# Down projection of a streaming encoder: later bias preparation, another order of the three form slots, and the last part of x added in DRAM

## The chip, the cores and the metric

The kernel runs on one core of a Trainium2 chip. A core has a matrix engine (PE, with its weight loads shown as PEld), a vector engine (DVE), a scalar engine (ACT), a general engine (POOL, which also issues DMAs) and SP, which only issues DMAs. Each engine works through its own list of instructions in order; so does each DMA queue's issuer. The metric is the device time of one launch in microseconds (us), lower is better.

## The reference, cut to what matters

One step of a hybrid encoder, here with one layer of each of its two kinds; all in float32, for 1024 prompt frames and 8 x 16 sample frames (nine tiles of 128 rows, D = 1024).

```python
def rmsnorm(x, g):
    return x * rsqrt(mean(x * x, -1) + 1e-6) * g

def mlp(x, g_norm, w_up, w_down):            # w_up 1024x4096, w_down 4096x1024
    return square(relu(rmsnorm(x, g_norm) @ w_up)) @ w_down

# layer 0: sliding-window attention with distance penalty and sinks
hp = hp + band_attention(...) @ w_o_a
hp = hp + mlp(hp, g_mlp[0], w_up[0], w_down[0])
# layer 1: shared K/V, own queries, learned bias on the clipped distance
k_b, v_b = shared_kv(hp, g_kv, w_kv, g_k_b)
s = q @ k_b.T / 8 + table[clip(q_pos - k_pos, -128, 128) + 128]
hp = hp + softmax(s) @ v_b @ w_o_b
hp = hp + mlp(hp, g_mlp[1], w_up[1], w_down[1])   # hp, hs are outputs
```

## The kernel before

Each of the two layers runs `attention`, `wo_phase`, `mlp_up` and `mlp_down`. A float32 product is done as three products of rounded parts (high x high, high x low, low x high: `mm3`), so every operand is first split: ACT writes the high part, DVE the rest (`split`, L128 and L134).

`mlp_down` multiplies the 4096-wide activations by `w_down` with a scheme that needs 20 block products where plain blocking needs 24, run twice over (two halves `s` of the inner dimension): 40 **products**, numbered n = 0 to 39, in an order that `CHAINS` fixes. A product reads a **form** (a combination of activation blocks that `mlp_up` left in DRAM as `hd`) and a combination of weight blocks. It has three PSUM banks of 12 matmuls each, 36 matmuls in all.

- Forms come by SP (`load_h`, L1023) into three slots a0, a1, a2, 768 KB each. `slot(n)` is n % 3, but slot 1 for n = 39. A slot can be loaded again when the product that reads it has ended; at the end of iteration n the loop issues the next form whose slot is not claimed by a nearer one. Then ACT casts the form (L128) and DVE makes its low part (L134).
- Weight blocks come by SP into r slots (1 MB each, `load_w`). `add_w` sums two of them on DVE (L1059) two products ahead; `split_w` splits the sum (ACT L128, DVE L134) one product ahead. All loads of this function are held in one order by `self.sp`; most of its DVE work is held in one order by `self.dve` (`chain`). Everything else is ordered by a scheduler that takes ready instructions by program order, with a lead of 1000 for the start of the next layer's attention.
- The result has three **parts** of three token tiles each (part 0 is tiles 5, 6, 7; part 1 is 2, 3, 4; part 2 is the sample tile, 0, 1), each in two column halves. Where a part's x tiles aren't open yet, a bank is copied by ACT into an o slot (L1151) and added to DRAM (`xp`) by one accumulating DMA of POOL (L1165, 768 KB). Part 2 is opened after product 1 and part 1 after product 12 (`X_AT`): their first write is an ACT copy (L1157), later ones DVE adds (L1159); when the last has come, POOL adds each tile (512 KB) to DRAM (L1092), after product 30 for part 2, 35 for part 1. Part 0 (`HELD`) is opened after product 34 by three SP loads of x from DRAM; products 37 (left half) and 39 (right half) are added by DVE, and SP stores the tiles (L1090). In the second layer POOL also copies parts 1 and 2 from DRAM to the output (L1170) three products after their end.

The nine x tiles, the slots and the next layer's attention share SBUF; a tile of the next stage can be written once every old tile under it is given back. Counted from the pools of the program, in bytes per partition: x5, x6, x7 lie at 52800 to 65088, x8 and x0 (part 2) at 91200 to 99392, x1 at 118336 to 122432; a0 at 106048, a1 at 138816, a2 at 151104, each 12288 long. In the second layer's attention, the normed and transposed first tile `hh` lies at 92224 to 96320 and `hl` at 96320 to 100416 (written at L128 and L134 from `ps_n`), a bias tile `biasB` at 116800, `gk`, `gq` at 120896, the first piece of the second tile at 121920; the weights `wq` over x6 and x7. In `mlp_up`, the first sum of x (`sx0`) lies under a0 and is last read by the first product of the last block; under a2 lie `sx4` and the sample's x8, last read when the sample products of that block have ended.

`prep_bias` (L1185) prepares the second layer's distance bias while the first layer's `mlp_down` runs: it loads a table (`tb`), clears `fr` and `big` and makes differences on DVE, stores `fr` to `fd`, writes it 128 times over to `rd` in DRAM (3072 KB, L1196), then gathers 16 pieces of `rd` into `big` (L1210, L1212) and stores that (`biasSd`). In the program it stands ahead of product 20 (`RANK`), but nothing orders it.

At the seam of the layers the second layer's first loads and splits (`w_kv` by L146, POOL L185, DVE L190) stand between the last products; after product 39 PE transposes x (L210), `hh` and `hl` are split, and the K/V products begin (L217 to L219).

Of the kernel before, what the change touches and what calls it, by code (L numbers as in the profile page):

```python
# [16 lines left out]
P = 128  # L17
# [6 lines left out]
KV = 4  # L24
# [70 lines left out]
class Build:  # L95
# [869 lines left out]
    def mlp_down(self, layer, out):  # L965
# [3 lines left out]
        with ExitStack() as st:  # L969
# [46 lines left out]
            last = {i // 2: max(left[i], left[i ^ 1]) for i in left}  # L1016
            aa, ws = {}, {}

            def slot(n):
                return 1 if n == total - 1 else n % 3  # L1020
# [57 lines left out]
            fresh_x = set()  # L1078

            def start_x(i):  # L1080
                for t in PARTS[i]:
                    xs[t] = take(f"x{t}")
                    if i == HELD:
                        load(xs[t], self.xd[t])
                    else:
                        fresh_x.update((t, h) for h in range(2))

            def store_x(i, t):
                if i == HELD:
                    nc.sync.dma_start(out(t), xs[t])  # L1090
                    return
                nc.gpsimd.dma_start(self.xd[t], xs[t], accum_op=ALU.add)  # L1092
                if out(t) is not self.xd[t]:
                    copies.append((n + 3, t))

            copies = []
# [22 lines left out]
            for n, (s, p, g, first, final, reads, _) in enumerate(seq):  # L1119
                if layer == 0 and n == RANK:  # L1120
                    self.prep_bias(self.dp)
                if n + AHEAD < total:
                    load_w(n + AHEAD)
# [8 lines left out]
                adds = {}  # L1132
                for o, v in reads:
                    if PARTS[o // 2][0] not in xs:
                        adds[o] = take(f"o{no % 2}")
                        no += 1
                for i in range(3):
# [11 lines left out]
                    for o, v in reads:  # L1149
                        if o in adds:  # L1150
                            nc.scalar.activation(adds[o][:, i], banks[i], AF.Copy, scale=float(v))  # L1151
# [3 lines left out]
                        if (t, o % 2) in fresh_x:  # L1155
                            fresh_x.remove((t, o % 2))
                            nc.scalar.activation(x, banks[i], AF.Copy, scale=float(v))  # L1157
                            continue
                        chain(tt(x, x, banks[i], ALU.add if v > 0 else ALU.subtract))  # L1159
                    for part in {o // 2 for o, _ in reads}:  # L1160
                        if last[part] == n:
                            store_x(part, PARTS[part][i])
                for o, z in adds.items():
                    dst = self.xp[o // 2][:, :, N[o % 2]].rearrange("t p n -> p t n")
                    nc.gpsimd.dma_start(dst, z, accum_op=ALU.add)  # L1165
                if n in X_AT:
                    start_x(X_AT[n])
                for m, t in copies:
# [719 lines left out]
```

## Time and profile before

| | us |
|---|---|
| median of 3 runs | 2364.53 (2361.72 to 2369.41) |
| the profiled execution, whole | 2373.72 |
| its span, first to last instruction | 2371.9 |
| PE busy in the span | 2284.4 |
| first layer's `mlp_down`, products 0 to 39 | 804.5 to 1150.4 |
| its products 20 and 37 begin at | 976.9 and 1117.5 |
| second layer's, products 0 to 39 | 2032.4 to 2367.5 |

The page gives busy times, the chain of work that ended last, and the costliest groups. "[2.69 <-DVE w L134]" behind a row of the timeline is idle time of the engine ahead of that instruction and what ended it. In the rows of the chain the columns are start, length, what. A row of the table by stretches gives for each engine the busy time and, in brackets, the number of instructions that began there, then PEclk (the granted clock of PE, 1.00 is full), the DMA engines' busy share and GB/s.

### The profile page before, as it was taken

The numbers are of one execution on the slowest core, as the hardware profiler recorded it, in microseconds if no ns is written. First come the engines' busy times: TensorE is split into PE (matmuls) and PEld (weight loads), VectorE is DVE, ScalarE is ACT, GpSimd is POOL, SyncE is SP. The second block draws the span as 40 slices with busy tenths as digits, with TensorE's granted clock in tenths as the row PEclk, the third lists the DMA queues.
The fourth block names the chain that finished last, engine by engine and source line by source line (L and its number), as shares of the span: only waits on it lengthen the run. The fifth ranks groups of instructions, "written<-read, shape, count | busy, mean of one in ns | idle before, by whom it ended". The sixth has DMA issues, their size and how long they took to land.

```text
span 2371.9 us, 33381 instructions
## 1 busy us (share of the span) xinstructions
PE 2284.4 (96%) x11429; PEld 1903.3 (80%) x11429; DVE 1723.7 (73%) x3084; ACT 1326.7 (56%) x2675; POOL 626.0 (26%) x938
## 2 busy tenths in 40 slices
PE   7998999899999999999999999998899999999998
PEld 6787877788888877887777788877788888888887
DVE  6788786666656578898577876777665565678886
ACT  3777675555555555444377666665555555554442
POOL 4334332313213111002233434344132132210010
PEclk9999999999999999999999999999999999999999
DMA  7335546234434798649553655555244343977465
GB/s 253 116 118 161 177 141 208 83 121 161 136 113 153 219 270 191 212 129 240 184 157 109 198 151 175 171 165 182 65 158 137 116 156 111 286 202 210 168 176 170
DMA packets 226042, 394.27 MB, mean 166 GB/s; under 512 B 51496, under 2 KB 126192, under 8 KB 225776
## 3 DMA queue, kind: packets, MB, share of 16 engines
q1 hardware_dynamic: 189680, 288.30, 38.1%
q0 software_dynamic: 34896, 99.11, 15.1%
q10 hardware_dynamic: 1296, 4.72, 0.5%
q8 instruction: 90, 1.47, 0.3%
q14 instruction: 80, 0.66, 0.1%
HBM read 238.08 MB, written 156.07 MB: 166 GB/s over the span
## 4 chain that ended last, share of the span: by engine, by line
PE 72%; DVE 9%; DMA 8%; ACT 4%; issue 4%; POOL 2%; SPq 0%; ACTq 0%; POOLq 0%; DVEq 0%
PE ps_c L743 6%; PE ps_c L744 6%; PE ps_c L745 6%; PE ps_x L743 5%; PE ps_x L745 5%; PE ps_x L744 5%; PE ps_mm L217 3%; PE ps_mm L219 3%; PE ps_mm L218 3%; DMA a<-hd 3%; PE ps_y L745 2%; PE ps_y L743 2%; PE ps_y L744 2%; PE ps_tr L324 2%; DVE w L134 2%
## 5 line engine op out<-in xcount | busy, mean ns | idle before, releaser
L743 PE MATMUL ps_c<-w,a 128*128 128x512 f32 x960 | 377.1, 393 | 8.8 <-DVE x L1159 5.7
L744 PE MATMUL ps_c<-w,a 128*128 128x512 f32 x960 | 376.6, 392 | 8.6 <-DVE w L134 8.6
L745 PE MATMUL ps_c<-w,a 128*128 128x512 f32 x960 | 375.9, 392 | 0.0
L908 POOL DMA_DIRECT2D hd<-h x272 | 148.8, 550 | 595.7 <-ACT h L817 373.5
L743 PEld LDWEIGHTS ps_c<-w,a 128*128 128x128 f32 x960 | 181.7, 189 | 51.2 <-DVE x L1159 5.7
L744 PEld LDWEIGHTS ps_c<-w,a 128*128 128x128 f32 x960 | 181.7, 189 | 48.2 <-DVE w L134 10.7
L128 ACT CAST a<-a 128x1536 fp32r<-128x1536 f32 x80 | 118.6, 1483 | 167.3 <-DMA a<-hd 167.3
L745 PEld LDWEIGHTS ps_c<-w,a 128*128 128x128 f32 x960 | 181.7, 189 | 37.9
L134 DVE TENSOR_TENSOR a<-a 128x1536 fp32r<-128x1536 f32 x80 | 140.2, 1753 | 63.9 <-ACT a L128 63.6
L217 PE MATMUL ps_mm<-w,hh 128*128 128x512 f32 x432 | 173.9, 404 | 6.4 <-POOL w L185 2.5
L219 PE MATMUL ps_mm<-w,hl 128*128 128x512 f32 x432 | 173.2, 402 | 2.1 <-DMA hl<-hTd 1.9
L218 PE MATMUL ps_mm<-w,hh 128*128 128x512 f32 x432 | 172.4, 400 | 1.7 <-DVE w L190 1.6
L743 PE MATMUL ps_x<-sx,w 128*128 128x512 f32 (+1 forms) x408 | 159.4, 391 | 3.5 <-ACT h L864 2.5
L128 ACT CAST w<-ru 128x512 fp32r<-128x512 f32 (+1 forms) x160 | 110.0, 708 | 83.7 <-PE ps_y L744 32.0
L745 PE MATMUL ps_x<-sx,w 128*128 128x512 f32 (+1 forms) x408 | 155.7, 382 | 0.0
L744 PE MATMUL ps_x<-sx,w 128*128 128x512 f32 (+1 forms) x408 | 155.6, 381 | 0.0
L128 ACT CAST w<-s 128x2048 fp32r<-128x2048 f32 x56 | 107.1, 1913 | 86.6 <-DVE s L1059 75.8
L134 DVE TENSOR_TENSOR w<-s,w 128x2048 fp32r<-128x2048 f32 x56 | 128.1, 2288 | 31.8 <-ACT w L128 30.8
L1165 POOL DMA_DIRECT2D xp<-o x28 | 36.1, 1289 | 419.0 <-ACT o L1151 407.9
L134 DVE TENSOR_TENSOR ptl<-ps_tr,pth 128x512 fp32r<-128x512 f32 x180 | 122.3, 685 | 26.4 <-ACT pth L128 20.7
L134 DVE TENSOR_TENSOR w<-ru,w 128x512 fp32r<-128x512 f32 (+1 forms) x160 | 126.6, 793 | 14.7 <-ACT w L128 14.6
L816 ACT ACTIVATE h<-h 128x512 f32<-128x512 f32 (+1 forms) x102 | 61.9, 607 | 123.3 <-DVE h L866 93.3
(271 smaller groups left out, 6135.5 us busy)
## 6 DMA issues: line engine op xcount, KB each, us to landing
a<-hd SPq DMA_DIRECT2D x80, 768.0 KB, 5.3
hd<-h POOLq DMA_DIRECT2D x272, 192.0 KB, 2.5
ru<-in_w_up SPq DMA_DIRECT2D x64, 512.0 KB, 4.0
r<-in_w_down SPq DMA_DIRECT2D x32, 1024.0 KB, 11.0
xp<-o POOLq DMA_DIRECT2D x28, 768.0 KB, 9.5
x<-xp SPq DMA_DIRECT2D x29, 512.0 KB, 4.6
o<-oTd SPq DMA_DIRECT2D x50, 256.0 KB, 5.3
xp<-xo SPq DMA_DIRECT2D x18, 512.0 KB, 2.9
```

The costliest lines, as they stand in the source:

```text
L128: a = nc.scalar.copy(hi, src)
L134: return a, e.tensor_tensor(lo, src, hi.bitcast(F32), ALU.subtract)
L217: nc.tensor.matmul(ps, a, w[:, 0, k, :], start=(k == 0), stop=False)
L218: nc.tensor.matmul(ps, a, w[:, 1, k, :], start=False, stop=False)
L219: self.lp = nc.tensor.matmul(ps, b, w[:, 0, k, :], start=False, stop=(k == KC - 1))
L324: self.lp = nc.tensor.transpose(pt[:, i, :], get(i), self.ident)
L743: a = mm(ps, ah, bh, start=first, stop=False, skip_group_check=True)
L744: mm(ps, ah, bl, start=False, stop=False, skip_group_check=True)
L745: return a, mm(ps, al, bh, start=False, stop=last, skip_group_check=True)
L816: a = nc.scalar.activation(t, src, AF.Relu)
L908: return lambda p, z: self.nc.gpsimd.dma_start(self.hd[c // 4][:, p, c % 4], z)
L1165: nc.gpsimd.dma_start(dst, z, accum_op=ALU.add)
```

## The change

Bias preparation: the table's load follows the last load of forms or weights that was issued, the two clears follow the DVE chain (so none can run ahead of product 20), `big` is cleared with them, and the 16 gathers and the store of `biasSd` become `spread_bias`, called ahead of product 24, each gather after the last load issued by then.

Form slots: n % 3 throughout; in the first layer turned by one, so that products 0, 1, 2 use a2, a0, a1 and 37, 38, 39 use a0, a1, a2. In the second layer 37, 38, 39 use a1, a2, a0.

Part 0: in the first layer it is never opened. ACT copies each bank of products 37 and 39 into the matching half of x8, x0, x1 (part 2's tiles, stored after product 30), and POOL adds that half (256 KB) to DRAM: six accumulating DMAs in the place of three loads, six DVE adds and three SP stores. In the second layer only the left half (product 37) goes that way, and POOL copies it to the output at iteration 38; the right half is loaded after product 33, added by DVE at product 39 and stored by SP, 256 KB a tile.

```diff
@@ -1013,11 +1013,12 @@
             for n, (s, *_, reads, _) in enumerate(seq):
                 for i, _ in reads:
                     left[i] = n
-            last = {i // 2: max(left[i], left[i ^ 1]) for i in left}
+            last = [max(left[2 * i], left[2 * i + 1]) for i in range(3)]
+            opened = {}
             aa, ws = {}, {}
 
             def slot(n):
-                return 1 if n == total - 1 else n % 3
+                return n % 3 if layer else (n + 2) % 3
 
             def load(dst, src):
                 a = nc.sync.dma_start(dst, src)
@@ -1075,25 +1076,28 @@
             def early(n):
                 return self.tc.high_priority(EARLY[n]) if n < len(EARLY) else nullcontext()
 
-            fresh_x = set()
-
-            def start_x(i):
-                for t in PARTS[i]:
-                    xs[t] = take(f"x{t}")
-                    if i == HELD:
-                        load(xs[t], self.xd[t])
-                    else:
-                        fresh_x.update((t, h) for h in range(2))
-
-            def store_x(i, t):
-                if i == HELD:
-                    nc.sync.dma_start(out(t), xs[t])
-                    return
-                nc.gpsimd.dma_start(self.xd[t], xs[t], accum_op=ALU.add)
-                if out(t) is not self.xd[t]:
-                    copies.append((n + 3, t))
-
-            copies = []
+            def start_x(n):
+                for o in X_AT[layer].get(n, ()):
+                    opened[o] = n
+                    for t in PARTS[o // 2]:
+                        if t not in xs:
+                            xs[t] = take(f"x{t}")
+                        if o == HELD:
+                            load(xs[t][:, N[o % 2]], self.xd[t][:, N[o % 2]])
+
+            def store_x(o, t):
+                if o == HELD and o in opened:
+                    nc.sync.dma_start(out(t)[:, N[1]], xs[t][:, N[1]])
+                elif o // 2 and last[o // 2] == n:
+                    nc.gpsimd.dma_start(self.xd[t], xs[t], accum_op=ALU.add)
+
+            def copy_x(n):
+                for part in range(3):
+                    for t in PARTS[part] if layer else ():
+                        if part and last[part] + 3 == n:
+                            nc.gpsimd.dma_start(out(t), self.xd[t])
+                        elif not part and left[0] + 1 == n:
+                            nc.gpsimd.dma_start(out(t)[:, N[0]], self.xd[t][:, N[0]])
 
             for n in range(AHEAD):
                 with early(n):
@@ -1119,6 +1123,8 @@
             for n, (s, p, g, first, final, reads, _) in enumerate(seq):
                 if layer == 0 and n == RANK:
                     self.prep_bias(self.dp)
+                if layer == 0 and n == RANK + 4:
+                    self.spread_bias(self.dp)
                 if n + AHEAD < total:
                     load_w(n + AHEAD)
                 split_h(n + 1)
@@ -1129,10 +1135,15 @@
                 if first:
                     banks = [self.psum("c", [P, 512], "ps_c") for _ in range(3)]
                 a, w = aa.pop(n), ws.pop(n)
-                adds = {}
+                adds, whole = {}, {}
                 for o, v in reads:
-                    if PARTS[o // 2][0] not in xs:
-                        adds[o] = take(f"o{no % 2}")
+                    if o not in opened:
+                        if n > max(last[1:]) + 1:
+                            adds[o] = [xs[t][:, N[o % 2]] for t in PARTS[2]]
+                            continue
+                        z = take(f"o{no % 2}")
+                        adds[o] = [z[:, i] for i in range(3)]
+                        whole[o] = z
                         no += 1
                 for i in range(3):
                     if i == 2 and n + 2 in total_of:
@@ -1148,26 +1159,26 @@
                     self.follow(z[0][0], z[-1][1])
                     for o, v in reads:
                         if o in adds:
-                            nc.scalar.activation(adds[o][:, i], banks[i], AF.Copy, scale=float(v))
+                            nc.scalar.activation(adds[o][i], banks[i], AF.Copy, scale=float(v))
+                            if o not in whole:
+                                dst = self.xd[PARTS[o // 2][i]][:, N[o % 2]]
+                                nc.gpsimd.dma_start(dst, adds[o][i], accum_op=ALU.add)
                             continue
                         t = PARTS[o // 2][i]
                         x = xs[t][:, N[o % 2]]
-                        if (t, o % 2) in fresh_x:
-                            fresh_x.remove((t, o % 2))
+                        if opened[o] is not None and o != HELD:
                             nc.scalar.activation(x, banks[i], AF.Copy, scale=float(v))
+                            if i == 2:
+                                opened[o] = None
                             continue
                         chain(tt(x, x, banks[i], ALU.add if v > 0 else ALU.subtract))
-                    for part in {o // 2 for o, _ in reads}:
-                        if last[part] == n:
-                            store_x(part, PARTS[part][i])
-                for o, z in adds.items():
+                    for o in {o // 2: o for o, _ in reads if left[o] == n}.values():
+                        store_x(o, PARTS[o // 2][i])
+                for o, z in whole.items():
                     dst = self.xp[o // 2][:, :, N[o % 2]].rearrange("t p n -> p t n")
                     nc.gpsimd.dma_start(dst, z, accum_op=ALU.add)
-                if n in X_AT:
-                    start_x(X_AT[n])
-                for m, t in copies:
-                    if m == n:
-                        nc.gpsimd.dma_start(out(t), self.xd[t])
+                start_x(n)
+                copy_x(n)
                 for _, z in zip(range(LATER), late):
                     chain(z)
                 for m in range(n + 1, total):
@@ -1185,8 +1196,10 @@
         nc = self.nc
         with ExitStack() as st:
             tb, fr, big = self.tb, self.fr, self.big
-            nc.sync.dma_start(tb, self.ins["rel_bias_b"][0])
-            nc.vector.memset(fr, 0.0)
+            a = nc.sync.dma_start(tb, self.ins["rel_bias_b"][0])
+            self.behind(self.sp, a)
+            self.behind(self.dve, nc.vector.memset(fr, 0.0))
+            self.behind(self.dve, nc.vector.memset(big, BIG))
             nc.vector.tensor_scalar(
                 fr[:, 127:383], tb[:, 256:0:-1], -1.0, tb[:, 256:257], ALU.mult, ALU.add
             )
@@ -1203,15 +1216,20 @@
                 )
 
             self.fsrc = fsrc
-            nc.vector.memset(big, BIG)
-            for h4 in range(G):
-                for b in range(2):
-                    r = slice(h4 * 32 + b * 16, h4 * 32 + b * 16 + 16)
-                    nc.sync.dma_start(big[r, :, b * P : b * P + P], fsrc(h4, 0, 16, KV, G, P))
-                    c = 256 + b * 16
-                    nc.sync.dma_start(big[r, :, c : c + 16], fsrc(h4, P, 16, KV, G, 16))
-            self.biasSd = dp.tile([KV, P, 288], F32, tag="biasSd", name="biasSd")
-            nc.sync.dma_start(self.biasSd[0:KV].rearrange("j p c -> p j c"), big)
+
+    def spread_bias(self, dp):
+        nc, big, fsrc = self.nc, self.big, self.fsrc
+        for h4 in range(G):
+            for b in range(2):
+                r = slice(h4 * 32 + b * 16, h4 * 32 + b * 16 + 16)
+                c = 256 + b * 16
+                for z in (
+                    nc.sync.dma_start(big[r, :, b * P : b * P + P], fsrc(h4, 0, 16, KV, G, P)),
+                    nc.sync.dma_start(big[r, :, c : c + 16], fsrc(h4, P, 16, KV, G, 16)),
+                ):
+                    self.behind(self.sp, z)
+        self.biasSd = dp.tile([KV, P, 288], F32, tag="biasSd", name="biasSd")
+        nc.sync.dma_start(self.biasSd[0:KV].rearrange("j p c -> p j c"), big)
 
     def prep_gains(self):
         nc, I = self.nc, self.ins
@@ -1831,8 +1849,8 @@
 TAIL = 6
 LATER = 3
 AHEAD = 3
-X_AT = {1: 2, 12: 1, 34: 0}
-HELD = 0
+X_AT = ({1: (4, 5), 12: (2, 3)}, {1: (4, 5), 12: (2, 3), 33: (1,)})
+HELD = 1
 WO_ORDER = [[0, 4, 1, 5, 2, 6, 7, 3, ST], [0, 4, 1, 5, 6, 2, 7, 3, ST]]
 
 CFG = [
```

## Prediction

> **What bounds the kernel now.** I read the page first, then the chain of waits, then tables by stretches around every product of the two down projections.
>
> ```profile
> span 2371.9 us, 33381 instructions
> PE 2284.4 (96%) x11429; PEld 1903.3 (80%) x11429; DVE 1723.7 (73%) x3084; ACT 1326.7 (56%) x2675; POOL 626.0 (26%) x938
> PE 72%; DVE 9%; DMA 8%; ACT 4%; issue 4%; POOL 2%; SPq 0%; ACTq 0%; POOLq 0%; DVEq 0%
> ```
>
> PE is the bound, and the chain of waits leaves it for 28% of the span: there another engine or a transfer sets the pace. The change touches only the down projections and the seam behind the first one, so I looked for products that are longer than the rest.
>
> ```profile
> core 0: us, PE busy (x) PEld busy (x) DVE busy (x) ACT busy (x) POOL busy (x), PEclk, DMA share, GB/s
> 870.46:878.62 8.16, 8.16 (x38) 6.76 (x37) 4.61 (x3) 3.11 (x3) 0.00 (x0) 1.00 1.01 297
> 878.62:911.58 32.96, 26.55 (x109) 21.24 (x108) 19.18 (x12) 15.84 (x16) 3.86 (x3) 0.95 0.87 217
> 1108.89:1131.85 22.96, 19.83 (x73) 15.41 (x73) 20.16 (x18) 6.82 (x6) 8.31 (x10) 0.85 0.88 244
> 1140.02:1150.41 10.39, 8.57 (x37) 6.81 (x37) 3.85 (x4) 0.00 (x0) 0.00 (x0) 1.00 0.31 112
> 2354.57:2367.50 12.93, 10.24 (x37) 7.67 (x35) 4.40 (x4) 0.00 (x0) 0.00 (x0) 0.87 0.19 77
> ```
>
> The first row is an undisturbed product (8 of the first layer): 8.16 us. The others: products 9 to 11, 8.48 above three such; 36 and 37, 6.64 above two; 39 of the first layer, 2.23 above one; 39 of the second, 4.77 above one, with PE idle for only 2.69 of it: the rest is clock (PEclk 0.87).
>
> **The change part by part.** The sum is made against the profiled execution (span 2371.9, whole 2373.72, 9.2 above the median 2364.53); I carry the difference over to the median.
>
> *The last product of the second layer.*
>
> ```profile
> 2346.61 5.49 DMA a<-hd
> 2352.12 1.49 ACT a L128
> 2353.63 1.76 DVE a L134
> 2355.39 2.21 DVE w L134
> ...
> 2367.54 0.69 DVE x L1159
> ```
> ```profile
> 2344.56 2.28 DVE L1059 TENSOR_TENSOR r<-r,r 128x2048 f32<-128x2048 f32 x1
> ```
> ```profile
> 2357.65 0.50 PE L744 MATMUL ps_c<-w,a 128*128 128x512 f32 x1 [2.69 <-DVE w L134]
> ```
>
> Form 39 shares slot 1 with product 37 and is loaded when that has ended; load, cast and two low parts make 10.95 us, more than product 38's 8.16. With three slots it follows product 36, one product earlier (at the end of 36, 2346.41 - 8.16 = 2338.3), lands by 2343.8 and is cast by 2345.3. The weights' sum ends at 2346.84; ACT's cast of it (near 2 us) and the two low parts, 1.76 and 2.21, are done by some 2352.8, ahead of 2354.57, where the product begins. What is late next is nothing until PE itself. Of 4.77 some 0.2 is the end of the last matmul: **-4.5**, and nothing in the queue can undo it (ends -4.6 and -3.5).
>
> A sentence of the Trainium skill speaks against the clock's share: TensorE: Matmul & The Clock Gate, section Why this matters for your kernels, names idle gaps over some 3 us as what drops the clock. Here 2.69 us idle already comes with a granted clock of 0.87, so the trace disagrees; by the rule this term would be an estimated -2.9.
>
> *The last store* moves 256 KB a tile, not 512. The last add ends at 2368.23, the span 3.67 later; the smallest near row is 2.5 (hd<-h, below). **-0.5** (ends -1.2 and 0). The left half's accumulation (512 KB take 8.9, below) and its copy fall under products 38 and 39, 16 us of cover; without it they would stand behind the end, at 8.9 and more.
>
> *Product 39 of the first layer* waits for the same load: **-2.2** (ends -2.2 and 0, if DVE is held by the seam's work instead).
>
> *Product 37 of the first layer.*
>
> ```profile
> 1104.76 1.18 DVE L190 SCALAR_TENSOR_TENSOR w<-raw,gcol,w 128x512 fp32r<-128x512 f32 x1 [1.50 <-POOL w L185]
> ...
> 1116.90 1.84 DVE L190 SCALAR_TENSOR_TENSOR w<-raw,gcol,w 128x512 fp32r<-128x512 f32 x2 [0.68 <-POOL w L185]
> 1118.67 2.28 DVE L134 TENSOR_TENSOR w<-r,w 128x2048 fp32r<-128x2048 f32 x1
> ```
>
> The next layer's weight splits (L190) stand on DVE ahead of w(36) and w(37), and DVE stood 1.50 us for POOL, which waited for the w_kv load; that load stood behind the three x loads (1.5 MB), which go. So w(37) comes up to 1.50 earlier, and product 37's wait, of at least 1.5, roughly halves; clock losses shrink faster than waits (2.23 above for the first layer's 39, 4.77 for the second's). A full working gives -4.2; the order on DVE may differ, so I take **-3.0** (ends -6.6, all of it, and +3, as much again as the wait).
>
> *The bias preparation.*
>
> ```profile
> 870.69 14.81 DMA a<-hd
> 885.52 1.49 ACT a L128
> 887.03 1.76 DVE a L134
> 888.79 2.20 DVE w L134
> ```
> ```profile
> 865.88 0.32 SPq L1194 DMA_DIRECT2D fd<-fr  x1
> 867.38 0.60 SPq L1196 DMA_DIRECT2D rd<-fd  x1
> ...
> 882.63 0.33 SPq L1210 DMA_DIRECT2D big<-rd  x1
> ...
> 896.09 0.44 SPq L1212 DMA_DIRECT2D big<-rd  x1
> ...
> 901.85 0.38 SPq L1214 DMA_DIRECT2D biasSd<-big  x1
> ```
> ```profile
> L1189 DVE MEMSET fr<- x1: 378/378/378, 862.1 to 862.1; 16x384 f32 x1
> ...
> L1206 DVE MEMSET big<- x1: 1018/1018/1018, 862.7 to 862.7; 128x1152 f32 x1
> ...
> L1190 DVE TENSOR_SCALAR fr<-tb x1: 336/336/336, 865.5 to 865.5; 16x256 f32<-16x256 f32 x1
> ```
> ```profile
> 978.31 0.69 DVE L1159 TENSOR_TENSOR x<-x,ps_c 128x512 f32<-128x512 f32 x1 [4.53 <-ACT x L1157]
> ...
> 981.12 0.68 DVE L1159 TENSOR_TENSOR x<-x,ps_c 128x512 f32<-128x512 f32 x1
> ...
> 1007.46 0.68 DVE L1159 TENSOR_TENSOR x<-x,ps_c 128x512 f32<-128x512 f32 x1
> ```
>
> Although it stands at product 20, it ran at product 7: rd is written in 15 us (867.38 to the first gather at 882.63), form 10 lands only 2.9 us behind it, and products 9 to 11 lose 8.48. Tied down, it runs from product 20 on (976.9 here). There DVE works almost without a gap from 978.31 to 1007.46, so the two clears and the difference, 0.38 + 1.02 + 0.34 = 1.74 us, come straight on the path of w(21) to w(23); ahead of them stands the add at 981.12, so fr is ready near T20 + 6.7 (T20: begin of product 20) and rd goes out near T20 + 8.4. SP's next form, 23, becomes free for issue at the same time. If it goes behind rd it lands near T20 + 25 (form 10 landed 18.1 after rd went out, with the DMA engines full; a little less here). Product 23 could begin at T20 + 3 x 8.16 + 1.74 = T20 + 26.2, and cast and low parts (1.49 + 1.76 + 2.2) want the form 5.5 ahead of that, at T20 + 20.8: 4.2 us of wait and, as in the second layer's last product, some 1.6 of clock. The 16 gathers take SP 13.5 us (882.63 to 896.09) from product 24 on and push form 27, due at 8.16, by 5.3 us. Its slack is two products less load and parts, 16.3 - 5.5 - 5.5 = 5.3: 0.2. biasSd waits until 901.85, another 5.3 on SP; behind it stands form 28, whose place comes up by then. Sum after: 1.74 + 4.2 + 1.6 + 0.2 = 7.7, against 8.48: **-0.8**. Bounds: 2.0 if form 23 goes first (-6.5); form 27 behind biasSd as well (+6: 5.3 of wait and some clock). The nearest row is this same transfer, so I stay by it.
>
> *The seam.*
>
> ```profile
> 1151.05 2.08 ACT L128 CAST hh<-ps_n 128x512 fp32r<-128x512 f32 x4 [11.08 <-PE ps_n L210]
> ```
> ```profile
> 1152.20 0.48 PE L217 MATMUL ps_mm<-w,hh 128*128 128x512 f32 x1
> ```
> ```profile
> hd<-h POOLq DMA_DIRECT2D x272, 192.0 KB, 2.5
> ...
> xp<-x POOLq DMA_DIRECT2D x12, 512.0 KB, 8.9
> ```
>
> Here the change adds a wait. hh and hl lie on x8 and x0. Before, these tiles were given back after product 30, and the cast ran 0.64 us behind product 39 (end E = 1150.41). Now x0 carries bank 1 of product 39: its matmuls end at E - 2.7 (a third of a product), a copy like DVE's 0.69 ends near E - 1.8, and POOL's accumulation must land first. No 256 KB accumulation is in the trace; it lies between 2.5 (192 KB, plain) and 8.9 (512 KB, added): I take 5, between the two. So hh is free near E + 3.2, the K/V products begin near E + 4.6 instead of E + 1.8: 2.8, and 1.2 of clock for a PE pause of that length (1.9 stood behind 2.69): **+4.0** (ends +1 and +9). Behind the cast ACT holds only later tiles; behind gk and gq on SP (x1, free near E + 6) stand the w_q loads, which are needed after the K/V products of three tiles only.
>
> *The first products of the first layer.*
>
> ```profile
> 788.14 8.64 DMA a<-hd
> ```
> ```profile
> 793.31 0.40 PE L743 MATMUL ps_x<-sx,w 128*128 128x512 f32 x1
> ```
>
> Form 0 goes to a2 and must wait for the end of the sample products (793.31), 5.2 us later than 788.14. But the 1 MB ahead of it has then landed: 5.5 as in the calm load above, so 798.8 against 796.8. Cast and low parts, 5.5, end at 804.3; product 0 began at 804.5. It just fits: **+0.3** (ends 0 and +2).
>
> The first layer's six ACT copies and POOL issues in the place of DVE adds lie beside PE's products 37 to 39, where ACT is idle for most of the time (0.00 busy in the last product's row).
>
> Sum: -4.5 - 0.5 - 2.2 - 3.0 - 0.8 + 4.0 + 0.3 = **-6.7**, so 2364.5 - 6.7 = 2357.8.
>
> **The rivals.** *The bias finds a gap* (form 23 ahead of rd): -6.5 for -0.8, sum -12.4, 2352.1. For: the two are ready within 1 us of each other. Against: rd stands first in the program.
>
> *The wait only changes its place:* product 37 stays as it is and the seam costs 9 (an accumulation like the 8.9 row): -4.5 - 0.5 - 2.2 - 0.8 + 9 + 0.3 = +1.3, 2365.8. Then the change doesn't do what it says for the first layer. For: most accumulations of the page take that long. Against: DMA share 0.31 in the last product.
>
> *Slower, by POOL's queue.* The accumulations of product 37 wait on POOL for ACT; if the scheduler puts w_kv's splits (L185) behind them, DVE's L190 wait for POOL, and w(38) and w(39) stand behind those: two stalls like that of 37 (about 6.2 each, 6.64 with product 36's share), 37 itself as before. That is two times 6.2 for 38 and 39, of which 2.2 was there before at 39: -4.5 - 0.5 - 0.8 + 4 + 0.3 + 12.4 - 2.2 = +8.7, 2373.2. It decides from the point where a split block is queued behind bank 2 of product 37. For: the 1.50 and 0.68 waits above are of this kind. Against: the splits have a lead of 1000 in the order.
>
> **How the numbers follow.** Forecast 0.44, with its own range 2352 to 2363; bias in a gap 0.24; changed place 0.16; slower 0.16. A measurement of this kernel can tell about 0.3% (7.1 us) from no change, so the forecast itself lies on that edge: 0.23 of it faster, 0.21 within. Faster 0.23 + 0.24 = 0.47; within 0.21 + 0.16 = 0.37; slower 0.16. The range leaves out the slower case beyond 2369 and, below 2348, a gap for the bias together with all of product 37.
>
> **What would show it.** Second layer's product 39: 8.2 us, form 39 issued a product earlier. First layer: products 9 to 11 at 8.2 to 9; MEMSET rows behind the adds of product 19; a form that lands 3 us behind rd, and a long product 23 or 24. Seam: the cast of hh waiting for an xp DMA. Wrong would be a form 39 still late, hh written at once, or a long product 38.

## The result, and the profile after

| | median us | runs | |
|---|---|---|---|
| before | 2365.07 | 17 (2360.66 to 2371.67) | |
| after | 2358.24 | 17 (2353.62 to 2362.03) | ratio 0.9968, 95% interval 0.9957 to 0.9978 |

The change saves 0.22 to 0.43%, 5 to 10 us; the forecast was 6.7 (2357.8). The two profiles differ by more, 19.7 us of span, and most of the surplus must not be put down to the change: the profile of before is a long one (2373.72, above the 17 runs in the table), that of after a short one (2354.01), and the first `mlp_down` alone begins 5.0 earlier (804.49 and 799.51), upstream of every edit but the form slots. So I compare stretches, not spans. The page of the changed kernel, its head and the first line of the chain:

```profile
span 2352.2 us, 33396 instructions
...
PE 2271.4 (97%) x11429; PEld 1893.3 (80%) x11429; DVE 1715.4 (73%) x3075; ACT 1332.4 (57%) x2684; POOL 635.3 (27%) x950
...
PE 74%; DVE 9%; DMA 9%; ACT 3%; issue 3%; POOL 1%; SPq 0%; ACTq 0%; DVEq 0%; POOLq 0%
```

The chain is on PE for 74% instead of 72%. The table by stretches of the changed kernel (columns as before): products 0 and 1, 9 to 11, 20 to 28, 37 and 39 of the first layer, and 39 of the second.

```profile
799.51:817.45 17.94, 16.62 (x74) 13.44 (x73) 14.86 (x13) 10.45 (x12) 4.05 (x6) 1.00 0.93 311
875.03:899.51 24.48, 24.48 (x109) 20.27 (x108) 19.35 (x12) 14.93 (x15) 3.88 (x3) 1.00 0.99 234
964.79:1044.12 79.33, 74.86 (x325) 60.43 (x324) 72.89 (x59) 32.56 (x23) 0.00 (x0) 1.00 0.55 182
1111.24:1123.54 12.30, 10.08 (x37) 7.85 (x36) 10.92 (x6) 4.28 (x4) 0.85 (x1) 0.86 1.03 281
1131.70:1140.03 8.33, 8.33 (x39) 6.87 (x38) 0.00 (x0) 1.20 (x2) 1.71 (x2) 1.00 0.32 36
2339.77:2348.09 8.32, 8.32 (x37) 6.57 (x35) 1.37 (x2) 0.00 (x0) 1.12 (x2) 1.00 0.70 156
```

The same view of before for products 0 and 1 and products 20 to 28:

```profile
804.49:821.13 16.64, 16.61 (x74) 13.44 (x72) 13.75 (x13) 9.97 (x12) 4.05 (x6) 1.00 0.99 323
976.86:1051.67 74.81, 73.98 (x326) 60.66 (x324) 71.44 (x56) 33.28 (x23) 0.00 (x0) 1.00 0.41 138
```

Products 9 to 11 are now three plain products (24.48), where they took 32.96: -8.5. Products 20 to 28 pay for it with 79.33 instead of 74.81: +4.5. Both last products are plain again: 8.33 for 10.55, both counted to the end of the last matmul (the 10.39 of the table before ends with PE's first transpose), and 8.32 for 12.93, while products 0 and 1 take 1.3 more. The timeline of after round the broadcast, engine by engine (start, length, what, idle time before), shows why 20 to 28 are longer:

```profile
969.27 0.38 DVE L1201 MEMSET fr<- 16x384 f32 x1
969.84 1.02 DVE L1202 MEMSET big<- 128x1152 f32 x1 [0.19 <-issue]
...
997.41 1.76 DVE L134 TENSOR_TENSOR a<-a 128x1536 fp32r<-128x1536 f32 x1 [4.75 <-ACT a L128]
```
```profile
973.14 0.34 SPq L1024 DMA_DIRECT2D a<-hd  x1
...
978.72 0.60 SPq L1209 DMA_DIRECT2D rd<-fd  x1
983.03 0.33 SPq L1024 DMA_DIRECT2D a<-hd  x1
```

The clears stand ahead of product 21's low parts (that product takes 9.84). Form 23 went out at 973.14, **ahead** of the broadcast; the form behind it is 24, issued 983.03, and DVE idles 4.75 for that form's cast. At the seam:

```profile
1142.63 1.07 ACT L128 CAST hh<-ps_n 128x512 fp32r<-128x512 f32 x2 [1.96 <-DMA xp<-x]
...
1143.33 0.19 PEld L217 LDWEIGHTS ps_mm<-w,hh 128*128 128x128 f32 x1 [1.75 <-issue]
1143.36 0.47 PE L217 MATMUL ps_mm<-w,hh 128*128 128x512 f32 x1 [1.55 <-ACT hh L128]
```

The cast of `hh` waits 1.96 for an accumulation, as forecast, and PE 1.55 for the cast; from PE's first transpose (1139.87) to the first K/V product are 3.49 us, before 1.79. The delay lasts: the 96th K/V matmul (`ps_mm`) begins 26.53 behind that transpose, before 24.62.

### The profile page after: what moved, and what is told of

Read it like the earlier page. It is cut to its first block, busy times and chain, and to the rows that moved or that the text cites. A ratio compares the mean times of both kernels' runs of the same rounds, so it can differ in the third digit from the quotient of the medians.

```text
span 2352.2 us, 33396 instructions
## 1 busy us (share of the span) xinstructions
PE 2271.4 (97%) x11429; PEld 1893.3 (80%) x11429; DVE 1715.4 (73%) x3075; ACT 1332.4 (57%) x2684; POOL 635.3 (27%) x950
## 3 DMA queue, kind: packets, MB, share of 16 engines
q0 software_dynamic: 36432, 102.26, 15.9%
## 4 chain that ended last, share of the span: by engine, by line
PE 74%; DVE 9%; DMA 9%; ACT 3%; issue 3%; POOL 1%; SPq 0%; ACTq 0%; DVEq 0%; POOLq 0%
PE ps_c L743 6%; PE ps_c L744 6%; PE ps_c L745 6%; PE ps_x L743 5%; PE ps_x L745 5%; PE ps_x L744 5%; PE ps_mm L217 3%; PE ps_mm L219 3%; PE ps_mm L218 3%; PE ps_y L745 2%; PE ps_y L743 2%; PE ps_y L744 2%; PE ps_tr L324 2%; DMA a<-hd 2%; DVE w L134 1%
```

## Experiments

Every time is against the kernel before on the same chip. The first table gives what was timed; the second is from one profile each. In the second, a product lasts from its first matmul to that of the next one (product 39 to the end of its last matmul), and each number is the sum over the products named less 8.16 for each; "seam" is the time from the first L210 to the first K/V product.

| kernel | median us | before | ratio, 95% interval |
|---|---|---|---|
| slots alone | 2362.30 | 2367.94 | 0.9975, 0.9962 to 0.9988 |
| bias alone | 2366.27 | 2367.94 | 0.9991, 0.9977 to 1.0005 |
| part 0 alone | 2376.52 | 2367.94 | 1.0034, 1.0021 to 1.0048 |
| after, part 0 in its own tiles | 2357.36 | 2367.94 | 0.9953, 0.9936 to 0.9969 |
| after, bias at product 12 | 2355.53 | 2367.63 | 0.9957, 0.9945 to 0.9970 |
| after, old bias | 2362.30 | 2367.63 | 0.9988, 0.9975 to 1.0001 |
| after, x1 kept | 2363.66 | 2367.63 | 0.9987, 0.9971 to 1.0002 |
| after, broadcast in halves | 2360.05 | 2367.63 | 0.9965, 0.9952 to 0.9978 |
| after, n % 3 throughout | 2359.02 | 2368.53 | 0.9954, 0.9937 to 0.9971 |
| after, product 12 and halves | 2355.68 | 2368.53 | 0.9939, 0.9922 to 0.9956 |
| the same, n % 3 throughout | 2353.10 | 2368.53 | 0.9932, 0.9916 to 0.9948 |
| the same, own tiles | 2352.46 | 2368.53 | 0.9935, 0.9919 to 0.9952 |

| first layer, above 8.16 | 0, 1 | 9-11 | 12-19 | 20-28 | 35-37 | 38 | 39 | seam |
|---|---|---|---|---|---|---|---|---|
| before | 0.3 | 8.5 | 0 | 1.4 | 6.7 | 0 | 2.4 | 1.8 |
| after | 1.6 | 0 | 0 | 5.9 | 6.0 | 0 | 0.2 | 3.5 |
| slots alone | 1.6 | 10.7 | 0 | 0.7 | 7.0 | 0 | 2.2 | 1.8 |
| bias alone | 0.5 | 0 | 0 | 6.6 | 5.7 | 1.0 | 4.0 | 1.8 |
| part 0 alone | 0.4 | 8.7 | 0 | 0.7 | 4.7 | 4.2 | 6.4 | 3.2 |
| own tiles | 1.6 | 0 | 0 | 8.3 | 3.7 | 0 | 1.7 | 1.7 |
| bias at 12 | 1.7 | 0 | 6.0 | 0 | 4.6 | 0 | 1.5 | 3.2 |
| old bias | 1.6 | 10.3 | 0 | 0.9 | 5.9 | 0 | 1.1 | 3.4 |
| x1 kept | 1.8 | 0 | 0 | 5.6 | 4.1 | 0 | 1.1 | 1.7 |
| halves | 1.8 | 0 | 0 | 5.8 | 4.5 | 0 | 1.4 | 3.3 |
| n % 3 | 0.4 | 0 | 0 | 8.3 | 4.7 | 0 | 0.2 | 3.4 |
| 12 and halves | 1.7 | 0 | 0 | 0.1 | 5.9 | 0 | 0.2 | 3.2 |
| the same, n % 3 | 0.5 | 0 | 0 | 0.2 | 4.6 | 0 | 0.2 | 3.5 |
| the same, own tiles | 1.4 | 0 | 1.3 | 1.0 | 5.6 | 0 | 0.4 | 1.7 |

### The slots alone

```diff
-                return 1 if n == total - 1 else n % 3
+                return n % 3 if layer else (n + 2) % 3
```

> The kernel before with the new slot order alone. Theory P (each piece keeps the size it has in the profile of the changed kernel): product 39 of the second layer 8.3 us instead of 12.9 (-4.6), product 39 of the first layer 8.3 instead of 10.6 (-2.2), product 0 of the first layer 1.3 longer, because its form waits for the end of the sample products: together -5.5 against the kernel before. Theory I (the pieces depend on each other): form 38 and 39 of the first layer now stand a product earlier on SP, ahead of or between the three x loads and the w_kv loads that this kernel still has, so product 37 loses more than its 6.2; the first layer then gains nothing, and the sum is -3.3 or less of a gain.

The second layer's product 39 is 8.32 as expected, product 0 pays its 1.2, but the first layer's product 39 stays at 10.38: theory I's outcome, by another mechanism than it named. The timed gain, 0.12 to 0.38% or 3 to 9 us, holds the sums of both theories; it is the profile that decides. Of the kernel with the slots alone, the timeline of that stretch:

```profile
1138.86 1.06 ACT L201 ACTIVATE junk<-x 128x1024 bf16<-128x1024 f32 x1 [3.79 <-DMA x<-xp]
...
1139.91 1.89 ACT L128 CAST w<-r 128x2048 fp32r<-128x2048 f32 x1
...
1142.27 0.27 DVE L1605 MEMSET biasB<- 64x256 f32 x1 [2.08 <-DMA biasB<-rd]
...
1142.74 2.27 DVE L134 TENSOR_TENSOR w<-r,w 128x2048 fp32r<-128x2048 f32 x1
...
1145.07 0.50 PE L744 MATMUL ps_c<-w,a 128*128 128x512 f32 x1 [1.72 <-DVE w L134]
```

The form is there in time, but on ACT the statistics of the next attention's third x tile (L201) stand ahead of the cast of w(39), the weights of product 39, and wait 3.79 for that tile's load. The cast ends at 1141.80; on DVE the clear of the bias tile, which waits 2.08 for a load of its own, then holds the low part back to 1142.74. One wait took the place of the other.

### Part 0 alone

The kernel after with the old slot line and the old `prep_bias`.

> The kernel before with the new handling of part 0 alone (added in DRAM in the first layer, left half only in the second), old slots, old bias preparation. Theory P: last store -0.3, product 37 and its neighbours -0.8, seam +1.7: +0.6, which is no difference to be told. Theory I: with the old slots forms 38 and 39 are not issued early, the w_kv splits aren't pushed together on DVE ahead of w(37), and product 37 falls by 3 or more, as on record: -0.3 - 3.0 + 1.7 = -1.6; product 37 decides between them (12.3 by P, 11 or less by I).

This is slower, by 0.21 to 0.48%; neither theory has it. Product 37 falls as theory I says (10.75), but 38 and 39 lose 10.6 together, and the second layer's product 39 is long again (12.60). The timeline of part 0 alone, with the row of product 39 from the table by stretches:

```profile
1130.37 0.38 SPq L540 DMA_DIRECT2D kc<-in_cache_k_b  x1
...
1130.54 1.77 POOL L1163 DMA_DIRECT2D xp<-x  x2 [3.48 <-ACT x L1160]
...
1130.81 0.47 SPq L542 DMA_DIRECT2D vc<-in_cache_v_b  x1
...
1131.32 0.47 SPq L556 DMA_DIRECT2D ub<-biasSd  x1
...
1131.81 1.55 POOL L1163 DMA_DIRECT2D xp<-x  x1
...
1131.90 0.38 SPq L1024 DMA_DIRECT2D a<-hd  x1
...
1140.45 1.47 ACT L128 CAST a<-a 128x1536 fp32r<-128x1536 f32 x1 [5.91 <-DMA a<-hd]
...
1141.98 0.79 PE L743 MATMUL ps_c<-w,a 128*128 128x512 f32 x1 [3.35 <-ACT a L128]
...
1145.97 0.80 PE L744 MATMUL ps_c<-w,a 128*128 128x512 f32 x1 [3.20 <-DVE w L134]
```
```profile
1141.98:1156.57 14.59, 11.39 (x38) 8.83 (x39) 3.94 (x2) 1.20 (x2) 1.74 (x2) 0.69 0.18 20
```

As form 39 shares its slot with product 37, it can go out only when that has ended (1129.65). SP issues three small loads of the next attention first (`kc`, `vc`, `ub`), POOL the three accumulations of product 37, and the form goes out at 1131.90, 2.25 behind the end; it is cast 8.55 after its issue. In the kernel before, it went out 0.20 behind the end of product 37 (1131.85) and was cast 4.62 later. The DMA engines are 0.90 busy in the 8.55 us here and were 0.44 busy then (1132.10 to 1140.60), and two of the accumulations that went out beside the form took 9.8 and 10.4. That the accumulations slow the form is argued from this; no run separates them from the three small loads. PE stops twice (the first stop, ahead of product 39's first matmul, counts into product 38), and over product 39 the clock falls to 0.69.

### The bias alone

> The kernel before with the tied bias preparation alone. Theory P: products 9 to 11 at 8.16 each (-8.5), and products 20 to 28 some 5.9 above 8.16 each instead of 1.4 (+4.5), with form 23 issued ahead of the broadcast and form 24 the one that lands late: -4.0. Theory F (the order on record: form 23 goes behind the broadcast, and the gap in the changed kernel is luck of the turned slots): a wait of some 4 us at product 23 and a loss of 7.7 against 8.5, so -0.8.

The edit is `prep_bias`, `spread_bias` and its call. Products 9 to 11 are clean, products 20 to 28 cost 6.6 (theory P's pattern: form 23 goes out at 977.93, ahead of the broadcast at 982.74, and product 24 takes 12.66; so the gap in the changed kernel is no luck of the turned slots). In this profile products 38 and 39 lose 2.6 more than before. The interval reaches from a gain of 0.23% to a loss of 0.05%: alone, the tying buys little or nothing that can be told, and the sums of both theories lie inside.

### Slots and part 0 together

The kernel after with the old `prep_bias`.

> The changed kernel with the old, untied bias preparation: the new slots and the new part 0 together. Theory I (slots and part 0 need each other: with the old slots form 39 of the first layer comes behind six accumulations, and with the old part 0 the seam's work on ACT and DVE takes the place of the form): product 38 and 39 of the first layer at 8.2 to 8.4, as in the changed kernel, against 12.3 and 14.6 with part 0 alone and 10.4 with the slots alone, products 9 to 11 lose 8 to 10 again, and the sum is -3 to -5 against the kernel before, far from the +2 that the two measured alone add up to (-5.6 and +8.6). Theory S (the pieces simply add): +2.

Theory I: product 38 is 8.16 and 39 is 9.28, where part 0 alone has 12.33 and 14.59. The ratio, 0.9988, is below the 1.0009 that the two alone multiply to (0.9975 x 1.0034), and its interval leaves that out; but the 1.0009 is uncertain by about 0.2% itself, so the times lean to theory I, and products 38 and 39 decide. With three slots form 39 goes out ahead of the accumulations, and without the x loads less of the seam's work stands ahead of w(39); product 39 is still 0.9 longer than theory I has it.

This doesn't show that part 0 gains anything. Slots and part 0 together (0.9988) were measured no faster than the slots alone (0.9975), and by the profiles what products 35 to 39 gain from it (2.2) the seam takes back in large part (1.6). The kernel with the slots and the later bias but the old part 0 was not run.

### The seam

Part 0 copied into x5, x6, x7 in the first layer, and into x5, x6 and x1 (the diff is that of the first):

```diff
-                            adds[o] = [xs[t][:, N[o % 2]] for t in PARTS[2]]
+                            for t in PARTS[0] if layer == 0 else ():
+                                if t not in xs:
+                                    xs[t] = take(f"x{t}")
+                            adds[o] = [xs[t][:, N[o % 2]] for t in PARTS[0 if layer == 0 else 2]]
```

> The changed kernel, but in the first layer ACT copies part 0 into x5, x6, x7, which stand unused there, and not into x8, x0, x1, under which hh and hl lie. Theory P (the cast of hh waits for the accumulation that reads x0): the K/V products begin 1.8 us behind the end of product 39 instead of 3.5, so 1.7 less than the changed kernel, -8.5 against the kernel before. Theory Q (the wait only changes its place: w_q lies over x6 and x7, or POOL's queue holds the next thing): the seam as long as in the changed kernel, -6.8.

> The changed kernel, but in the first layer ACT copies part 0 into x5, x6 and x1: hh and hl lie under x8 and x0 alone, while gk, gq and the bias tile lie at x1. Theory G (x1, given back only after product 39, is what keeps gk, gq and the bias tile's clear off DVE ahead of w(39)): the K/V products begin 1.7 us behind product 39 as with all three own tiles, and product 39 stays at 8.3, where that kernel had 9.8: 1.7 less than the changed kernel, -8.5 against the kernel before. Theory H (it is the third x load's statistics on ACT, ahead of the cast of w(39)): product 39 is 9.8 again and the gain at the seam is lost.

Both bring the seam back to 1.70, so the accumulation under `hh` is what costs up to 1.8 there. Neither turns it into a gain of the whole that can be told. With all three own tiles, gk, gq and the bias tile are free early, and (timeline of that kernel) their DVE work waits for its load ahead of w(39):

```profile
1132.29 0.19 DVE L627 TENSOR_SCALAR gq<-gq 128x64 f32<-128x64 f32 x1 [2.10 <-DMA gq<-in_g_q_b]
...
1132.86 2.28 DVE L134 TENSOR_TENSOR w<-r,w 128x2048 fp32r<-128x2048 f32 x1
...
1135.20 0.50 PE L744 MATMUL ps_c<-w,a 128*128 128x512 f32 x1 [1.21 <-DVE w L134]
```

Product 39 is 1.5 longer than a plain one; what is gained at the seam stays (the 96th K/V matmul is 24.55 behind the first transpose, 26.53 in the changed kernel). With x1 kept, product 39 is 9.3, not the 8.3 of theory G, and the first tile's gain is followed by the second tile's cast, which then makes PE wait:

```profile
1151.95 0.50 PE L217 MATMUL ps_mm<-w,hh 128*128 128x512 f32 x1 [1.71 <-ACT hh L128]
```

The 96th K/V matmul is then 26.79 behind, so nothing of the gain is left.

The timed ratios (0.9953 and 0.9987, beside the changed kernel's 0.9968) don't separate either from it; product 39 between 8.3 and 9.6 is also what kernels with the same seam show (0.2 to 1.5 in the column).

### The broadcast, its place and its size

Three kernels: the broadcast in two halves (the second behind form 24), the preparation at product 12, and both (the second half behind form 16, at PREP + 2). For the whole broadcast at product 20 the kernel with n % 3 throughout stands beside them; its bias preparation is that of the change. The first diff is the broadcast in halves, the second the earlier place.

```diff
+                if layer == 0 and n == RANK + 2:
+                    half = P // 2
+                    z = nc.sync.dma_start(
+                        self.rd[0:H, half:], self.fd[0:H].unsqueeze(1).to_broadcast([H, half, 384])
+                    )
+                    self.behind(self.sp, z)
...
-            nc.sync.dma_start(rd, fd[0:H].unsqueeze(1).to_broadcast([H, P, 384]))
+            self.fd, self.rd = fd, rd
+            half = P // 2
+            nc.sync.dma_start(rd[0:H, 0:half], fd[0:H].unsqueeze(1).to_broadcast([H, half, 384]))
```
```diff
+PREP = 12
...
-                if layer == 0 and n == RANK:
+                if layer == 0 and n == PREP:
                     self.prep_bias(self.dp)
-                if layer == 0 and n == RANK + 4:
+                if layer == 0 and n == PREP + 4:
                     self.spread_bias(self.dp)
```

> The changed kernel with the broadcast of rd in two halves of 1536 KB, the second behind form 24. Theory B: form 24 now waits for 7.4 us of broadcast, not 15, and lands some 5 to 7 us earlier, so product 24 is 8.2 us (9.6 in the changed kernel's profile, 12.7 and 13.3 in the two others with the tied preparation); products 21 and 22 keep the 1.7 and 0.7 of the clears: 1.5 to 5 less than the changed kernel, -8 to -12 against the kernel before. Theory D (DVE's order, not the form, sets product 24: a's low part stands behind three adds): product 24 stays at 9.6 or more.

> The changed kernel with the bias preparation eight products earlier, at products 12 (table, clears, broadcast) and 16 (gathers), where DVE is busy for 3.7 to 7 of 8.16 us and the DMA engines are at 0.3 in products 14 and 16. Theory B (the price left is the broadcast ahead of a form plus clears in a stretch where DVE has no gap): at product 12 DVE hides the clears, a form that lands late by some 7 has 5 of slack, so products 12 to 19 lose 0 to 2 and products 20 to 28 go back to 1.4 above 8.16 each: 3 to 6 less than the changed kernel, -10 to -13 against the kernel before. Theory F (a form behind the broadcast is late wherever it stands): the loss of 4 us only moves to product 15 or 16, and the sum stays at -7.

> The changed kernel with the bias preparation at product 12, where DVE has room, and the broadcast in two halves, the second behind form 16. Theory B2 (the price has two parts: clears and differences on a full DVE, worth 3 to 4 at product 20 and nothing at 12; and a form behind 15 us of broadcast, worth 1.5 to 5.5 wherever it stands and nothing with halves): products 12 to 19 at 8.2 to 8.6, 20 to 28 at 8.2, so the first layer's products take 5 less than in the changed kernel: -11 to -12 against the kernel before, the fastest so far. Theory F2 (some transfer is late behind any part of the broadcast): a product of 10 us or more between 15 and 18, and -8 or above.

Halves at product 20 (timeline of that kernel): form 24 is cast 8.0 behind its issue and product 24 is a plain 8.16, as theory B has it.

```profile
983.64 0.60 SPq L1217 DMA_DIRECT2D rd<-fd  x1
...
987.94 0.33 SPq L1024 DMA_DIRECT2D a<-hd  x1
988.32 0.56 SPq L1128 DMA_DIRECT2D rd<-fd  x1
...
995.97 1.48 ACT L128 CAST a<-a 128x1536 fp32r<-128x1536 f32 x1 [3.21 <-DMA a<-hd]
```

With the whole broadcast it comes later; in the kernel with n % 3 throughout (timelines of SP, ACT and PE) 15.9 behind its issue, and the product waits 3.49:

```profile
982.03 0.60 SPq L1209 DMA_DIRECT2D rd<-fd  x1
986.36 0.33 SPq L1024 DMA_DIRECT2D a<-hd  x1
```
```profile
1002.29 1.48 ACT L128 CAST a<-a 128x1536 fp32r<-128x1536 f32 x1 [5.86 <-DMA a<-hd]
```
```profile
1007.82 0.79 PE L744 MATMUL ps_c<-w,a 128*128 128x512 f32 x1 [3.49 <-DVE w L134]
```

But halves alone save nothing in sum: products 25 to 27 take over what 24 gave up (5.8 against 5.9 for 20 to 28). At product 12 with the whole broadcast, DVE hides the clears, products 20 to 28 lose nothing, and the late form costs 6.0 at products 15 and 16 (13.71 for 16): theory F's outcome, and the slack of 5 that theory B counted on is not there (its timed interval, 0.9945 to 0.9970, holds the sums of both theories). Only both together remove the price (of the three profiles with both, two keep 0.1 and 0.2 of it, one 2.3). Of the kernel with both, products 12 to 19 and 20 to 28:

```profile
898.90:964.18 65.28, 65.28 (x289) 54.06 (x288) 55.50 (x37) 31.97 (x28) 3.83 (x3) 1.00 0.93 271
964.18:1037.70 73.52, 73.52 (x326) 60.75 (x325) 70.11 (x55) 33.56 (x22) 0.00 (x0) 1.00 0.43 147
```

65.28 is eight times 8.16, 73.52 is nine times it and 0.08.

### The turn of the slots, and the fastest versions

> The changed kernel with n % 3 in both layers: in the first layer products 0, 1, 2 use a0, a1, a2 as before, and 37, 38, 39 use a1, a2, a0. Theory T (the longer product 0, 9.6 instead of 8.4, is the price of the turn: form 0 in a2 waits for the end of the sample products): product 0 back at 8.4, products 37 to 39 as in the changed kernel (12.3, 8.2, 8.3 to 9.6), so 1.2 less: -8 against the kernel before. Theory U (the turn keeps a0 free at the seam, where a bias tile lies partly under it): product 0 gains 1.2, the seam or product 39 loses as much or more, and the sum stays at -7 or above.

> The same with n % 3 in both layers. Theory T: 1.2 less than with the turn, -12 to -13 against the kernel before. Theory U: no less than with the turn.

> The same (turned slots) with part 0 copied into x5, x6, x7 in the first layer. Theory P: the K/V products 1.5 to 1.7 behind product 39 instead of 3.3, which stays to the end: -13 against the kernel before. Theory H (gk, gq and the bias tile then come ahead of product 39 and their work on DVE, or the statistics on ACT, delays w(39) by as much as the seam gains): product 39 at 9.6 or more, the sum as without it, -11 to -12.

Without the turn, products 0 and 1 lose 0.4 and 0.5 instead of 1.4 to 1.8, and product 39 is as short: theory T for products 0 and 39. The column "seam" ends with the first K/V product, though: with n % 3 alone PE waits 1.49 more for the third x tile (1158.20), the 96th K/V matmul is 28.04 behind the first transpose instead of 26.53, which takes the gain back in this profile as theory U would have it. In the version with halves at product 12 and n % 3 it is 26.45, so that wait is not shown to come of the slots. The timed pairs (0.9954 and 0.9968, 0.9932 and 0.9939) lean the same way but overlap. With the own tiles the seam is 1.70, product 39 loses 0.4, but the broadcast's price is back in part (2.3 in products 12 to 28); the sum is again the same. The version with the preparation at 12, halves and n % 3 has an interval, 0.9916 to 0.9948, below that of the change, 0.9957 to 0.9978: it beats both kernels, the changed one by about 0.36% (0.9932 / 0.9968), 8.5 us, as two ratios taken against the kernel before on two occasions.

## Why the prediction was right, and where its steps were not

The time (2358.24 for 2357.8) is right, and that it is so close is in part luck. By pieces of the two profiles the sum is -4.6 - 0.3 - 2.2 - 0.8 - 4.0 + 1.7 + 1.3 = -8.9, inside the measured 5 to 10; four of the seven terms were off by 1 to 3, two each way, and mostly cancelled.

- **Second layer's product 39: -4.5, measured -4.6.** Right in mechanism too: form 39 goes out as product 37 begins, and with the new slots the product is 8.32 whatever else is changed; with the old ones 11.58 and 12.60.
- **Last store: -0.5, measured -0.3** (from the last matmul's end to the span's, 4.4 and 4.1).
- **First layer's product 39: -2.2, measured -2.2, by a step that is incomplete.** "Waits for the same load" was true of before, but the new slots alone leave 10.38. The end 0 of the term, "if DVE is held by the seam's work instead", is nearly what the slots give alone (-0.2), held on ACT more than on DVE; the product is short only where part 0 is also added in DRAM.
- **First layer's product 37: -3.0, measured -0.8** for 35 to 37. The step that failed is that w(37) comes up by 1.5 and nothing else moves. PE's wait in product 37 fell from 3.13 to 2.22, not by half. w(37)'s low part does start 0.9 earlier in its product (1111.52 against a begin of 1111.24; before 1118.67 against 1117.48), but with the loads gone the splits of `w_kv` come early too: three of them now stand ahead of w(36).

```profile
1096.02 3.38 DVE L190 SCALAR_TENSOR_TENSOR w<-raw,gcol,w 128x512 fp32r<-128x512 f32 x3
1099.32 2.28 DVE L134 TENSOR_TENSOR w<-r,w 128x2048 fp32r<-128x2048 f32 x1
...
1111.52 2.28 DVE L134 TENSOR_TENSOR w<-r,w 128x2048 fp32r<-128x2048 f32 x1
```

  Product 35 grew from 8.26 to 9.92 by that. Over all profiles with the new part 0, 35 to 37 cost 3.7 to 6.0, with the old one 5.7 to 7.0: the gain is about 1.5, and the clock decides the rest (below).
- **Bias preparation: -0.8, measured -4.0** in this pair of profiles (-8.5 + 4.5). The step that failed is "if it goes behind rd": form 23 went first, which was the rival's condition. But the rival's price, 2.0, failed as well: neither asked which form is next. Form 24 is, and it pays. Over the five kernels with the whole broadcast at product 20, products 20 to 28 cost 5.6 to 8.3. Of this the kernels with the old preparation have 0.7 to 1.4 as well, which the prediction left out, so the added cost is 4.2 to 7.6; the 7.7 on record lies at the upper end, for a form and a product that were named one too early. Products 9 to 11 in turn cost 8.5 to 10.7 in the four kernels with the old preparation.
- **Seam: +4.0, measured +1.7.** The mechanism is as put; both sizes were too large. The clock term (1.2) did not come: PE's pause was 1.55. And the accumulation that held `hh` landed faster than the 5 taken (4.15; the median of all six is):

```profile
xp<-x POOLq DMA_DIRECT2D x6, 256.0 KB, 4.1
```

- **First products: +0.3, measured +1.3**, within its bounds. "It just fits" was 1 us too kind.
- **The rival by POOL's queue** (slower, long products 38 and 39) did not happen in the changed kernel, but part 0 alone is slower in just these two products, by a form 39 that goes out late and lands slowly rather than by w_kv's splits behind POOL's accumulations.

What I did not settle is why the parts of the program outside the change differ by some 11 us (19.7 less 8.9) between the two profiles.

## What to carry to other kernels

When a large transfer is moved, ask which load goes out next behind it and what slack that one has; a quieter place hides the engine work around the transfer, and cutting it hides its length, and here only both together paid. An edit that is a loss alone need not be one beside another (part 0 alone costs 0.21 to 0.48%, beside the slots no cost can be told), so undo parts from the finished kernel as well as adding them to the old one. Freeing memory earlier can let the next stage's work in ahead of this stage's last steps.

## What was unexpected of the hardware

After a pause of PE of about 1.8 to 3 us the clock fell in some cases and not in others. In the fourteen profiles of this study, the down projections hold 64 waits of PE of 0.9 us or more inside a layer (idle time ahead of a matmul of `ps_c`). Among the 36 matmuls that follow such a wait I counted the long ones (over 0.45 us). Up to 1.7 us (29 waits) there was one at most, the first; between 1.7 and 3.0 us, 11 of 23 had one and 12 had 8 to 10; above 3.0 us all 12 had 7 to 14. In 9 of these 24 cases the long ones, but for the first, begin only with the third to seventh matmul, when PE is at work again. The counts hold inside the down projections only. In `mlp_up`, where shorter waits stand close ahead, a wait of 1.36 came with a clock of 0.57 over the next 8 us in the kernel before (from 447.30), one of 1.35 with 1.00 in the changed kernel (from 445.10). The same wait at product 37 shows the price, 12.30 in the changed kernel (clock 0.86) and 10.70 in the fastest version:

```profile
1113.86 0.50 PE L744 MATMUL ps_c<-w,a 128*128 128x512 f32 x1 [2.22 <-DVE w L134]
```
```profile
1111.01 0.50 PE L745 MATMUL ps_c<-w,a 128*128 128x512 f32 x1 [2.24 <-DVE w L135]
```
```profile
1108.38:1119.08 10.70, 8.46 (x37) 6.68 (x36) 10.31 (x6) 3.83 (x3) 0.85 (x1) 1.00 1.04 290
```

The Trainium skill (TensorE: Matmul & The Clock Gate, section Part 1: The HAM clock gate) describes a free-running window of about 3.4 us that must be idle for the clock to drop; that the same wait falls either way agrees with it, that waits from 1.81 us on can already cost it does not. The prediction took a clock loss behind a pause of 2.8 us at the seam as certain, where the runs give it an even chance.
